# Low parts of split weights: a VectorE subtraction, or a ScalarE copy and an accumulating transfer

## The chip, the cores and the metric

The kernel runs on one core of a Trainium2 chip. The metric is the device time of one execution in microseconds. Three runs of the kernel before took 1647.87, 1644.26 and 1647.29 us, median 1647.29. A core has TensorE (matmuls, PE in the profile, its weight loads PEld), VectorE (DVE), ScalarE (ACT), GpSimd (POOL) and SyncE (SP), each working through its own queue of instructions in order, and 16 DMA engines, which all queues of transfers share.

## The reference

A two-layer backbone over 512 latent tokens and 256 context tokens of width 1024, batch 1, in float32. Around every sub-layer stand RMS norms with a shift, a scale and a gate taken from a conditioning vector (adaLN).

```python
h = rmsnorm(x, norm_g[l, 0]) * (1.0 + sc1) + sh1          # latent, and context with its own shift and scale
# layer 0: z = h @ w_in; multi-scale pooling heads beside a two-way gated linear recurrence (HGRN2); concat @ w_out
# layer 1: grouped-query attention, 8 query heads on 2 key heads, normalised q and k, 2-D rotary positions; @ w_out
x = x + g1 * rmsnorm(y, norm_g[l, 1])
a, b = split((rmsnorm(x, norm_g[l, 2]) * (1.0 + sc2) + sh2) @ ffn_w_in[l])
x = x + g2 * rmsnorm((silu(a) * b) @ ffn_w_out[l], norm_g[l, 3])
```

The context stream is needed up to the keys and values of layer 1; the output is the latent stream, 512 x 1024. The FFN's hidden width is 2816.

## The kernel before

Activations lie transposed: channels on the 128 partitions, tokens along the columns. Large products are computed from split operands. Each float32 operand is held as two float32r tiles, a rounded one ("hi") and the rest ("lo"), and a product is the sum of three matmuls, hi·hi, hi·lo of the activation, and lo·hi of the weight (`mm3`, lines 121 to 123). TensorE needs both parts of a weight before it can finish a product.

Weights come in slots of 128 x 2048 (`wslot`). For each half slot of 128 x 1024 (512 KB), SP loads the raw weights into one of four `raw` tiles (line 102), ScalarE copies them, rounded, into the hi tile (line 573), and VectorE subtracts hi from raw into the lo tile (line 574, in `split`). Slots live in a pool of two (`whi`, `wlo`); in the FFNs every third slot goes to a third place (`w3hi`, `w3lo`), and the output projections have two more (`wohi`, `wolo`). There are 92 slots: the value projection of layer 0 (2), its input projection (10), its output projection (4), the FFN of layer 0 (33), the projections of layer 1 (6 with the values), its output projection (4), and the last FFN (33). A slot can be filled again only when TensorE has made its last matmul from it; a `raw` tile can be loaded again only when its reader is done.

```python
hi = pool.tile([128, 2048], F32R, tag=tag + "hi", name=tag + "hi")
for a in range(0, n, 1024):
    self.split(hi[:, a:b], lo[:, a:b], self.load(src[:, a:b], b - a)[:, :b - a], self.weng)
```

`split` is also used for activations (attention's keys, queries, probabilities, the FFN's hidden tiles); those calls are not touched.

The program is written stage after stage, with norms of the next stage let in between the matmuls of the last (`along`, `tick`). Norm chains (`sumsq`, `rms`, `spread`, `postnorm`, `prenorm`) run from ScalarE's squares over VectorE's sums (line 171), a small TensorE matmul (140), GpSimd's power (146) and a second small matmul (158) to VectorE's products (187, 229). GpSimd also adds the gated result to x (233) and, at the start, makes half of the low parts of the modulated input (215). The order of instructions on each engine is then set by the framework's scheduler, which goes by its own estimate of when operands are ready, and which adds the waits; so an edit in one place can change the order of all engines. During the FFN of layer 0, 48 further loads through the `raw` tiles feed the adaLN products of layer 1 on VectorE (line 299); during the mixer of layer 0, 32 such loads feed TensorE (line 277). SP's queue also carries the rotary transfers of layer 1 (`sw`, line 677).

Of the kernel before, what the change touches and what calls it, by code (L numbers as in the profile page):

```python
# [12 lines left out]
ALU = mybir.AluOpType  # L13
# [37 lines left out]
class Cols:  # L51
    """Tiles of context (256) and latent (512) columns by channel tile, addressed by column 0..768."""
# [8 lines left out]
class Groups:  # L61
    """256-column tiles by channel tile."""
# [19 lines left out]
class Trunk:  # L82
# [22 lines left out]
    def wslot(self, src, n, pool=None, tag="w"):  # L105
        """One slot of weights, split into two parts that add up to it exactly."""
        if pool is None:
            self.nw += 1
            pool, tag = (self.w3, "w3") if self.w3 and self.nw % 3 == 0 else (self.wp, "w")
        hi = pool.tile([128, 2048], F32R, tag=tag + "hi", name=tag + "hi")  # L110
        lo = pool.tile([128, 2048], F32R, tag=tag + "lo", name=tag + "lo")
        for a in range(0, n, 1024):
            b = min(n, a + 1024)
            self.split(hi[:, a:b], lo[:, a:b], self.load(src[:, a:b], b - a)[:, :b - a], self.weng)
        return hi, lo

    def mm3(self, out, ops, first=True, last=True):
        """Sum over k of w_k^T x_k from split operands (wh, wl, xh, xl)."""
        n = len(ops)
        for i, (wh, wl, xh, xl) in enumerate(ops):  # L120
            self.nc.tensor.matmul(out=out, lhsT=wh, rhs=xh, start=first and i == 0, stop=False)  # L121
            self.nc.tensor.matmul(out=out, lhsT=wh, rhs=xl, start=False, stop=False)  # L122
            self.nc.tensor.matmul(out=out, lhsT=wl, rhs=xh, start=False, stop=last and i == n - 1)  # L123
# [5 lines left out]
    def ops(self, w, o, h, a, b, k0=0, k1=KD):  # L129
        """Operands of mm3: blocks k0..k1 of weights from column o on against h's columns a..b."""  # L130
        return [(w[0][:, o + (k - k0) * 128:o + (k - k0 + 1) * 128], w[1][:, o + (k - k0) * 128:o + (k - k0 + 1) * 128],
                 h[0](k, a, b), h[1](k, a, b)) for k in range(k0, k1)]

    def rms(self, ss, n, count, tag="aux"):
        """rsqrt(sum over partitions of ss / count + eps) by column."""
        nc = self.nc
        nt = n // 128
        pc = self.ps(tag)
        for t in range(nt):
            nc.tensor.matmul(out=pc[:, 2 * t:2 * t + 2], lhsT=ss[:, t * 128:(t + 1) * 128], rhs=self.ones[:, 0:2],  # L140
                             start=True, stop=True)
        v = self.sm.tile([128, 6], F32, tag="rv", name="rv")
        nc.vector.tensor_scalar(out=v[:, :nt], in0=pc.rearrange("p (t two) -> p t two", two=2)[:, :nt, 0],  # L143
                                scalar1=1.0 / count, scalar2=EPS, op0=ALU.mult, op1=ALU.add)
        r = self.sm.tile([128, 6], F32, tag="rr", name="rr")
        nc.gpsimd.tensor_tensor(out=r[:, :nt], in0=v[:, :nt], in1=self.mhalf[:, :nt], op=ALU.pow)  # L146
        return r, n

    def spread(self, rn, tag="aux"):
        """What rms returned, on every partition: PSUM [128, n]."""  # L150
        nc = self.nc
        r, n = rn
        dg = self.sm.tile([128, 256], F32, tag="dg", name="dg")
        for t in range(n // 128):
            nc.vector.tensor_scalar(out=dg[:, t * 128:(t + 1) * 128], in0=self.ident, scalar1=r[:, t:t + 1],
                                    scalar2=None, op0=ALU.mult)
        pb = self.ps(tag)
        nc.tensor.matmul(out=pb[:, :n], lhsT=self.ones, rhs=dg[:, :n], start=True, stop=True)  # L158
        return pb
# [16 lines left out]
    def prenorm(self, x, h, l, which, a, b):  # L176
        """h = rmsnorm(x) * (1 + sc) + sh of the columns a..b (of one stream), in two parts."""
# [21 lines left out]
    def norm(self, x, a, b):  # L199
        """x = rmsnorm(x) without its gain, over the columns a..b."""  # L200
        ss = yield from self.sumsq(x, a, b)
        rb = self.spread(self.rms(ss, b - a, D))
        for k in range(KD):
            self.nc.vector.tensor_tensor(out=x(k, a, b), in0=x(k, a, b), in1=rb[:, :b - a], op=ALU.mult)

    def modulate(self, x, h, l, which, a, b):
        """h = x * (1 + sc) + sh of the columns a..b (of one stream) of a normalised x, in two parts."""
# [10 lines left out]
    def postnorm(self, x, y, l, which, a, b):  # L218
        """x += gate * rmsnorm(y) over the columns a..b (of one stream)."""
# [20 lines left out]
    def tick(self, us):  # L240
        """Emit the next parts of what goes along, for us of the main work."""
        self.credit = min(self.credit, 0.0) + us * RATE
        while self.bg and self.credit > 0:
            try:
                self.credit -= next(self.bg[0][1])
            except StopIteration:
                self.bg.pop(0)

    def advance(self, n=1):
        """Emit the next step of what waits for it."""  # L250
        for _ in range(n):
            self.pend = [g for g in self.pend if next(g, 0) is None]
# [5 lines left out]
    def finish(self, key=None):  # L258
        """Emit the rest of what goes along up to key (all of it without)."""
        while self.bg and (key is None or key in [k for k, _ in self.bg]):  # L260
            for _ in self.bg.pop(0)[1]:
                pass
# [19 lines left out]
    def ada_steps(self, n):  # L282
        """The next n of the steps that are left, which fill in between other work."""
# [10 lines left out]
    def ada_cols(self, m):  # L294
        """One tile of 128 columns of the modulation for both streams, by rows of the transposed weights."""
# [13 lines left out]
    def ada_tail(self, l, m0, m1, src):  # L309
        """Tiles m0..m1 of the modulation from what src has without the bias, and what follows from them."""  # L310
# [17 lines left out]
    def zslots(self, h, idx, evac):  # L328
        """Two 128-channel tiles of the input projection of layer 0 from one slot of weights."""
# [9 lines left out]
    def mixer0(self, hx, mx):  # L339
# [5 lines left out]
        def z_evac(h, d):  # L345
            """d = 0 forward, 1 backward: forget gates f (rows backward, forward) and k = 1 - f (forward, backward)."""
# [34 lines left out]
        def mixed(t, c):  # L381
            """[p, n, half, c] of a tile of two rows: the lower half of each block of 2c columns from the first row,
            the upper half from the second."""
# [3 lines left out]
        def hgrn(h):  # L387
            # Products of forget gates within blocks of c columns, c doubling: Q holds q times the product from the
            # block's start (forward) or to its end (backward), K holds k times the product of the rest of the block.
            # The pairs that meet at level c lie in the two halves of a block of 2c.  # L390
# [12 lines left out]
            def amm(kt, qt, w):  # L403
                """Products of the blocks of w columns: block g's keys with the columns qt(g), side by side by chunk."""
# [103 lines left out]
        def u_evac(g):  # L508
            w = POOL_WINDOWS[g]

            def f(pt, a, b):
# [4 lines left out]
                # columns: pad, context, pad, latent, pad  # L516
# [59 lines left out]
    def put(self, mx, k, s, e, src, scale=None):  # L576
        """Split src (times a column) into the operand tiles mx, columns s..e."""
# [23 lines left out]
    def ffn(self, l, y, h, order0, groups, last, done, step=0):  # L601
        """y = (silu(h w_a) * (h w_b)) w_out, hidden tiles in chunks; order0: the (tile, group) pairs to start with;
        the last chunk goes by the groups of last, each followed by done."""
# [67 lines left out]
    def rope(self, t, s):  # L671
        """Rotary positions of t [128, n], in place; s: its columns of the latent."""
# [9 lines left out]
    def att_proj(self, h, yp):  # L682
        """Queries (rotated, not yet normalised), their scales, and split keys and values."""
# [81 lines left out]
    def attention(self):  # L765
# [17 lines left out]
        def scores(u):  # L783
            """Softmax of 128 queries of a head over all keys."""
# [211 lines left out]
    def setup(self, cp):  # L996
# [20 lines left out]
        # lower bounds: row 0 of the softmax over the two rows  # L1017
# [20 lines left out]
def _cols(v):  # L1038
    """(..., n*128) -> [128, ... n]"""
# [4 lines left out]
def _tiles(w, cols):  # L1044
    """The 128-wide column tiles of w [K, N] named by cols: [len(cols), 128 p, K/128, 128]"""
# [5 lines left out]
def _pair(t):  # L1051
    """[2m, 128, k, 128] -> [m, 128, 2*k*128]"""
# [4 lines left out]
def pack(inp):  # L1057
# [5 lines left out]
    # ada: [l, sb, k, p, j, tile, 32]  # L1063
# [53 lines left out]
    # rotary tables: by channel of the head and latent token  # L1117
# [22 lines left out]
```

## Time and profile before

| | |
|---|---|
| runs | 1647.87, 1644.26, 1647.29 us; median 1647.29 |
| profiled execution, span from first to last instruction | 1643.8 us |
| TensorE busy | 1573.1 us (96%) |
| VectorE, ScalarE, GpSimd busy | 946.9, 587.2, 116.6 us |
| mean granted TensorE clock | 0.987 |
| read from HBM | 158.35 MB |
| DMA engines busy with queue 1 (SP's) | 31.7% of 16 engines |

The page gives no time of the profiled execution beside its span; the span lies 0.5 us below the fastest of the three runs and 3.5 us below their median. A busy share is an average over stages: in the attention, VectorE and ScalarE are nearly full, in the FFNs they are half idle. In the timelines a row gives start, duration, engine, line, the tiles written and read, and in brackets how long the engine sat idle before it and what ended that.

### The profile page before, as it was taken

The numbers are of one execution on the slowest core, as the hardware profiler recorded it, in microseconds if no ns is written. First come the engines' busy times: TensorE is split into PE (matmuls) and PEld (weight loads), VectorE is DVE, ScalarE is ACT, GpSimd is POOL, SyncE is SP. The second block draws the span as 40 slices with busy tenths as digits, with TensorE's granted clock in tenths as the row PEclk, the third lists the DMA queues.
The fourth block names the chain that finished last, engine by engine and source line by source line (L and its number), as shares of the span: only waits on it lengthen the run. The fifth ranks groups of instructions, "written<-read, shape, count | busy, mean of one in ns | idle before, by whom it ended". The sixth has DMA issues, their size and how long they took to land.

```text
span 1643.8 us, 26760 instructions
## 1 busy us (share of the span) xinstructions
PE 1573.1 (96%) x10842; PEld 1375.0 (84%) x10842; DVE 946.9 (58%) x1899; ACT 587.2 (36%) x1104; POOL 116.6 (7%) x147
## 2 busy tenths in 40 slices
PE   4999999999999999999999999999999999999997
PEld 1877776789898888888888898889998888888886
DVE  5557676655756566676532458778937523343345
ACT  3424343254542211212122134548845332222222
POOL 0200000001210000000000012320003000000002
PEclk9999999999999999999999999999999999999998
DMA  9242232342215444444321213230032223322311
GB/s 337 79 155 78 80 128 79 122 134 92 97 56 162 129 144 151 141 143 153 129 72 57 62 42 103 72 110 27 2 103 78 89 91 102 103 92 88 103 52 52
DMA packets 55803, 167.95 MB, mean 102 GB/s; under 512 B 7040, under 2 KB 16000, under 8 KB 55296
## 3 DMA queue, kind: packets, MB, share of 16 engines
q1 hardware_dynamic: 55536, 166.05, 31.7%
q8 instruction: 85, 1.39, 0.3%
q14 instruction: 38, 0.31, 0.1%
q10 hardware_dynamic: 144, 0.20, 0.0%
HBM read 158.35 MB, written 5.24 MB: 100 GB/s over the span
## 4 chain that ended last, share of the span: by engine, by line
PE 67%; DVE 5%; POOL 2%; issue 1%; ACT 1%; SPq 0%; DMA 0%; POOLq 0%; DVEq 0%; ACTq 0%
PE mm L121 21%; PE mm L122 21%; PE mm L123 21%; PE pp L819 1%; DVE ss L171 1%; DVE u L229 1%; PE aux L158 1%; POOL xl L233 1%; PE st L121 1%; PE st L123 1%; PE aux L140 1%; PE st L122 1%; POOL rr L146 1%; DVE wlo L574 1%; SPq L677 0%
## 5 line engine op out<-in xcount | busy, mean ns | idle before, releaser
L121 PE MATMUL mm<-hhl,whi 128*128 128x512 f32 (+1 forms) x944 | 326.8, 348 | 4.9 <-ACT kt L732 3.7
L123 PE MATMUL mm<-hhl,wlo 128*128 128x512 f32 (+1 forms) x944 | 326.8, 347 | 0.0
L122 PE MATMUL mm<-hll,whi 128*128 128x512 f32 (+1 forms) x944 | 326.4, 347 | 0.0
L573 ACT ACTIVATE whi<-raw 128x1024 fp32r<-128x1024 f32 x132 | 135.4, 1054 | 306.0 <-PE mm L122 243.7
L121 PEld LDWEIGHTS mm<-hhl,whi 128*128 128x128 f32 x944 | 180.1, 192 | 25.6 <-ACT kt L732 3.9
L123 PEld LDWEIGHTS mm<-hhl,wlo 128*128 128x128 f32 x944 | 180.3, 191 | 20.3
L122 PEld LDWEIGHTS mm<-hll,whi 128*128 128x128 f32 x944 | 180.6, 192 | 19.3
L624 DVE TENSOR_TENSOR sa<-sa,mm 128x512 f32<-128x512 f32 (+1 forms) x76 | 40.9, 539 | 270.0 <-PE mm L123 269.9
L574 DVE TENSOR_TENSOR wlo<-raw,whi 128x1024 fp32r<-128x1024 f32 x132 | 160.4, 1236 | 57.5 <-ACT whi L573 54.3
L146 POOL TENSOR_TENSOR rr<-rv,mhalf 128x2 f32<-128x2 f32 x55 | 45.6, 834 | 1471.8 <-DVE rv L143 1469.1
L299 DVE SCALAR_TENSOR_TENSOR junk<-raw,cb 128x1024 f32<-128x1024 f32 x96 | 117.3, 1222 | 44.4 <-DMA raw<-adat 43.5
L639 DVE TENSOR_TENSOR y<-y,mm 128x256 f32<-128x256 f32 x200 | 76.8, 417 | 90.5 <-PE mm L123 90.0
L123 PE MATMUL mm<-hhl,w3lo 128*128 128x512 f32 (+1 forms) x336 | 117.4, 350 | 0.0
L121 PE MATMUL mm<-hhl,w3hi 128*128 128x512 f32 (+1 forms) x336 | 117.4, 350 | 0.0
L122 PE MATMUL mm<-hll,w3hi 128*128 128x512 f32 (+1 forms) x336 | 117.2, 349 | 0.0
L121 PE MATMUL mm<-ghl,whi 128*128 128x512 f32 (+1 forms) x304 | 111.2, 371 | 1.3 <-DVE sa L624 1.3
L122 PE MATMUL mm<-gll,whi 128*128 128x512 f32 (+1 forms) x304 | 112.0, 370 | 0.4 <-DVE gll L574 0.4
L123 PE MATMUL mm<-ghl,wlo 128*128 128x512 f32 (+1 forms) x304 | 111.0, 367 | 0.0
L121 PE MATMUL mm<-hhc,whi 128*128 128x256 f32 x384 | 110.3, 291 | 0.1
L123 PE MATMUL mm<-hhc,wlo 128*128 128x256 f32 x384 | 109.5, 287 | 0.0
L122 PE MATMUL mm<-hlc,whi 128*128 128x256 f32 x384 | 108.3, 284 | 0.2 <-issue 0.2
L623 ACT ACTIVATE sa<-mm 128x512 f32<-128x512 f32 (+1 forms) x76 | 36.5, 480 | 159.0 <-PE mm L123 158.7
(227 smaller groups left out, 3319.1 us busy)
## 6 DMA issues: line engine op xcount, KB each, us to landing
raw<-w_fi SPq DMA_DIRECT2D x88, 512.0 KB, 3.9
raw<-ada SPq DMA_DIRECT2D x48, 512.0 KB, 5.3
raw<-adat SPq DMA_DIRECT2D x48, 512.0 KB, 3.7
raw<-w_fo SPq DMA_DIRECT2D x44, 512.0 KB, 4.0
raw<-w_ab SPq DMA_DIRECT2D x20, 512.0 KB, 4.4
raw<-w_at SPq DMA_DIRECT2D x10, 512.0 KB, 4.5
xl<-x SPq DMA_DIRECT2D x16, 256.0 KB, 5.2
raw<-w_abo SPq DMA_DIRECT2D x8, 512.0 KB, 4.3
```

Of the source, the lines that this page charges most:

```text
L121: self.nc.tensor.matmul(out=out, lhsT=wh, rhs=xh, start=first and i == 0, stop=False)
L122: self.nc.tensor.matmul(out=out, lhsT=wh, rhs=xl, start=False, stop=False)
L123: self.nc.tensor.matmul(out=out, lhsT=wl, rhs=xh, start=False, stop=last and i == n - 1)
L140: nc.tensor.matmul(out=pc[:, 2 * t:2 * t + 2], lhsT=ss[:, t * 128:(t + 1) * 128], rhs=self.ones[:, 0:2], start=True, stop=True)
L146: nc.gpsimd.tensor_tensor(out=r[:, :nt], in0=v[:, :nt], in1=self.mhalf[:, :nt], op=ALU.pow)
L158: nc.tensor.matmul(out=pb[:, :n], lhsT=self.ones, rhs=dg[:, :n], start=True, stop=True)
L299: nc.vector.scalar_tensor_tensor(out=self.junk, in0=raw, scalar=1.0, in1=self.cb[:, i * 1024:i * 1024 + 1024], op0=ALU.mult, op1=ALU.mult, ...
L573: self.nc.scalar.activation(out=hi, in_=src, func=AF.Copy)
L574: (eng or self.nc.vector).tensor_tensor(out=lo, in0=src, in1=hi.bitcast(F32), op=ALU.subtract)
L623: nc.scalar.activation(out=s[:, :n], in_=p[0][:, :n], func=AF.Silu)
L624: nc.vector.tensor_tensor(out=s[:, :n], in0=s[:, :n], in1=p[1][:, :n], op=ALU.mult)
L639: nc.vector.tensor_tensor(out=yt, in0=yt, in1=p, op=ALU.add)
```

## The change

In `wslot`, the low part of a half slot is made in another way. ScalarE writes a second copy of the raw weights, times -1, into the lo tile, rounded like the hi tile; then GpSimd issues a transfer inside SBUF from `raw` to `lo` that adds what it reads to what is there. The call of `split` is gone from `wslot`, and VectorE has no part in the weights any more. The other lines of the diff only remove comments; what follows `wslot` has line numbers higher by 3.

```diff
         for a in range(0, n, 1024):
             b = min(n, a + 1024)
-            self.split(hi[:, a:b], lo[:, a:b], self.load(src[:, a:b], b - a)[:, :b - a], self.weng)
+            raw = self.load(src[:, a:b], b - a)[:, :b - a]
+            self.nc.scalar.activation(out=hi[:, a:b], in_=raw, func=AF.Copy)
+            self.nc.scalar.activation(out=lo[:, a:b], in_=raw, func=AF.Copy, scale=-1.0)
+            self.nc.gpsimd.dma_start(out=lo[:, a:b], in_=raw, accum_op=ALU.add)
         return hi, lo
```

ScalarE's queue ahead of the value projection of layer 0, before; `hhc` are the rounded tiles of the modulated input:

```order
L573 ACTIVATE whi<-raw 128x1024
L214 ACTIVATE hhc_113<-u 128x256
L214 ACTIVATE hhc_114<-u 128x256
L214 ACTIVATE hhc_115<-u 128x256
L573 ACTIVATE whi<-raw 128x1024
L214 ACTIVATE hhc_116<-u 128x256
L214 ACTIVATE hhc_117<-u 128x256
L573 ACTIVATE whi<-raw 128x1024 x2
```

The same place now:

```order
L115 ACTIVATE whi<-raw 128x1024
L116 ACTIVATE wlo<-raw 128x1024
L115 ACTIVATE whi<-raw 128x1024
L116 ACTIVATE wlo<-raw 128x1024
L115 ACTIVATE whi<-raw 128x1024
L116 ACTIVATE wlo<-raw 128x1024
L115 ACTIVATE whi<-raw 128x1024
L116 ACTIVATE wlo<-raw 128x1024
L217 ACTIVATE hhc_113<-u 128x256
```

All eight weight copies now stand ahead of the first copy of the input, where one stood before.

GpSimd's queue at the same place now; before, the low parts `hlc` followed the powers at once:

```order
L149 TENSOR_TENSOR rr<-rv,mhalf 128x2 x3
L117 DMA wlo<-raw 128x1024 x4
L218 TENSOR_TENSOR hlc_130<-u,hhc_114 128x256
L218 TENSOR_TENSOR hlc_132<-u,hhc_116 128x256
L218 TENSOR_TENSOR hlc_134<-u,hhc_118 128x256
```

Four issues, each waiting for its second copy, now stand between the powers and the input's low parts.

TensorE's queue at the first slot of the FFN of layer 0, before (`w3hi`, `w3lo` are the slot's two parts):

```order
L158 MATMUL aux<-dg,ones 128x256
L121 MATMUL mm<-hhc_3727,w3hi 128x256
L122 MATMUL mm<-hlc_3743,w3hi 128x256
L123 MATMUL mm<-hhc_3727,w3lo 128x256
L121 MATMUL mm<-hhc_3728,w3hi 128x256
```

The same place now:

```order
L161 MATMUL aux<-dg,ones 128x256
L124 MATMUL mm<-hhc_3751,w3hi 128x256
L125 MATMUL mm<-hlc_3767,w3hi 128x256
L124 MATMUL mm<-hhc_3751,w3hi 128x256
L125 MATMUL mm<-hlc_3767,w3hi 128x256
L124 MATMUL mm<-hhl_3759,w3hi 128x256
L125 MATMUL mm<-hll_3775,w3hi 128x256
L124 MATMUL mm<-hhl_3759,w3hi 128x256
L125 MATMUL mm<-hll_3775,w3hi 128x256
L126 MATMUL mm<-hhc_3751,w3lo 128x256
```

The first matmul that reads the low part now comes after eight that don't, where two stood before; the matmuls of three further products have been drawn ahead.

## Rows read from the trace of the kernel before

**Rows 1.** The page: span, and busy time of each engine with its share.
```profile
span 1643.8 us, 26760 instructions
PE 1573.1 (96%) x10842; PEld 1375.0 (84%) x10842; DVE 946.9 (58%) x1899; ACT 587.2 (36%) x1104; POOL 116.6 (7%) x147
```

**Rows 2.** Instructions of the split by line: count, ns min/median/max, first and last start.
```profile
L573 ACT ACTIVATE whi<-raw x132: 1039/1058/1092, 37.7 to 1594.6; 128x1024 fp32r<-128x1024 f32 x132
...
L574 DVE TENSOR_TENSOR wlo<-raw,whi x132: 1184/1224/1760, 40.8 to 1595.9; 128x1024 fp32r<-128x1024 f32 x132
...
L574 DVE TENSOR_TENSOR w3lo<-raw,w3hi x44: 1216/1220/1226, 433.8 to 1585.0; 128x1024 fp32r<-128x1024 f32 x44
...
L574 DVE TENSOR_TENSOR wolo<-raw,wohi x8: 1215/1225/1227, 359.3 to 1206.3; 128x1024 fp32r<-128x1024 f32 x8
```

**Rows 3.** Timeline, last FFN: a slot's subtractions, and TensorE's first read of them.
```profile
1365.35 2.36 DVE L574 TENSOR_TENSOR wlo<-raw,whi 128x1024 fp32r<-128x1024 f32 x2
...
1386.72 0.39 PE L123 MATMUL mm<-ghl,wlo 128*128 128x512 f32 x1
```

**Rows 4.** The page's DMA queue 1, and DMA issues (count, size, us to landing).
```profile
q1 hardware_dynamic: 55536, 166.05, 31.7%
...
raw<-w_fi SPq DMA_DIRECT2D x88, 512.0 KB, 3.9
...
raw<-w_abv SPq DMA_DIRECT2D x4, 512.0 KB, 10.2
...
sw<-y SPq DMA_DIRECT2D x64, 32.0 KB, 1.9
```

**Rows 5.** Three stretches: us, busy time (count) by engine, PEclk, DMA share, GB/s.
```profile
0.00:40.00 40.00, 18.46 (x84) 6.02 (x84) 21.84 (x72) 15.18 (x33) 2.57 (x8) 0.96 0.93 345
354.00:434.00 80.00, 77.18 (x610) 74.32 (x610) 47.77 (x99) 44.90 (x98) 15.73 (x20) 1.00 0.41 139
1290.00:1605.00 315.00, 315.00 (x1466) 263.01 (x1465) 118.41 (x165) 85.27 (x116) 0.00 (x0) 1.00 0.30 94
```

**Rows 6.** Timeline, five places: rounded copies, and TensorE's first read of the low part.
```profile
74.99 2.01 ACT L573 ACTIVATE whi<-raw 128x1024 fp32r<-128x1024 f32 x2 [2.17 <-PE mm L123]
...
77.70 0.30 PE L123 MATMUL mm<-hhc,wlo 128*128 128x256 f32 x1
...
90.98 2.24 ACT L573 ACTIVATE whi<-raw 128x1024 fp32r<-128x1024 f32 x2 [0.50 <-DMA raw<-w_ab]
...
96.78 0.28 PE L123 MATMUL mm<-hhc,wlo 128*128 128x256 f32 x1
...
432.55 1.05 ACT L573 ACTIVATE w3hi<-raw 128x1024 fp32r<-128x1024 f32 x1
433.50 0.51 ACT L190 ACTIVATE hhl<-u,mods 128x256 fp32r<-128x256 f32 x1
...
435.04 0.38 PE L123 MATMUL mm<-hhc,w3lo 128*128 128x256 f32 x1 [0.89 <-DVE w3lo L574]
...
1027.15 1.06 ACT L573 ACTIVATE whi<-raw 128x1024 fp32r<-128x1024 f32 x1 [1.28 <-PE mm L122]
...
1031.26 0.28 PE L123 MATMUL mm<-hhl,wlo 128*128 128x256 f32 x1
...
1255.17 1.05 ACT L573 ACTIVATE w3hi<-raw 128x1024 fp32r<-128x1024 f32 x1
...
1259.37 0.28 PE L123 MATMUL mm<-hhl,w3lo 128*128 128x256 f32 x1
```

**Rows 7.** Timeline, the start: ScalarE's first weight copy and input copies, TensorE's first low-part wait.
```profile
37.68 1.06 ACT L573 ACTIVATE whi<-raw 128x1024 fp32r<-128x1024 f32 x1 [12.62 <-DMA raw<-w_abv]
...
39.15 1.06 ACT L214 ACTIVATE hhc<-u 128x256 fp32r<-128x256 f32 x3 [0.41 <-DVE u L212]
...
42.03 1.22 PE L122 MATMUL mm<-wlo,hhc 128*128 128x512 f32 x2 [1.68 <-DVE wlo L574]
```

**Rows 8.** Timeline, TensorE at the seam of FFN and layer 1.
```profile
1011.73 0.47 PE L140 MATMUL aux<-ones,ss 128*128 128x2 f32 x3 [2.24 <-DVE ss L171]
```

## The prediction, made before the changed kernel was run

> **What bounds the kernel now.** I read the busy shares first, then the split's own groups, then the timeline of each place where a split weight is first used. TensorE is busy for 1573.1 of the 1643.8 us of the span [rows 1]: the reader should see that any change can win at most the 71 us in which it is not, and that 21.5 of these lie in the first 40 us [rows 5], ahead of the first weight matmul, where no split has been needed yet. VectorE (947 us) and ScalarE (587 us) are far from full, so taking work from one and giving it to the other is worth nothing by itself. What counts is when a rounded weight or its low part becomes ready against when TensorE first reads it.
>
> The split is done 132 + 44 + 8 = 184 times, each on a half slot of 128x1024: a ScalarE copy of about 1.05 us, then a VectorE subtraction of about 1.22 us [rows 2]. In the steady part of the last FFN, the subtraction of a half slot starts at 1365.35 and takes 2.36 us with its neighbour, while TensorE reads the first half only at 1386.72 [rows 3]: some 20 us to spare. In the first FFN it is more. So most of the 92 slots can become ready several us later without anybody noticing. A few cannot, and they carry the forecast.
>
> **The change part by part.**
> Removed: 184 subtractions on VectorE, 184 x 1.22 = 224 us of busy time. Added on ScalarE: 184 further copies of the same shape as the rounded one, 184 x 1.05 = 193 us, which brings it to 780 us, below half of the span. Added on GpSimd: 184 DMA issues, in order with its own additions and powers. Added on the DMA engines: 184 transfers of 512 KB that read the raw weights and add to what lies in the low tile.
>
> *The price of one transfer.* No row of before shows an accumulating transfer, nor one issued by GpSimd. Nearest rows: a 32 KB transfer inside SBUF lands 1.9 us after its issue, a 512 KB load lands in 3.9 us, and in 10.2 us where four stand in a full queue [rows 4]. All of queue 1, 166.05 MB, takes 31.7% of 16 engines, which is 0.317 x 1643.8 / 166.05 x 0.524 = 1.65 us of all engines for 512 KB. The result needs two operands through the engines, the raw weights and minus the rounded ones, so I take two passes: 1.9 + 2 x 1.65 = 5.2 us, and 0.4 us for the issue, like SP's at its issues: 5.6 us in all. Lower bound 1.9 us, upper bound 10.6 us.
>
> On the price the Trainium skill says something too. In "DMA: Bandwidth & Descriptors", section "Anatomy of one DMA — SWDGE (gpsimd) path", it puts a GpSimd DMA at 2.0 us plus bytes over 436 GB/s, which is 3.2 us here, an estimate by that page; its term agrees with the 1.9 us of the small transfer [rows 4]. By it the sum below would shrink to almost nothing. The same page, under "Rules for kernel authors", says that an accumulating DMA reads its destination and writes it later, which no run here shows yet, and which would speak for the second pass.
>
> *The places with no room.* New ready time = end of the rounded copy + 1.06 us (the second copy) + 5.6. Against it stands TensorE's first read of the low part, later by what the new order puts in between, at 315.00 / 1466 = 0.215 us for a 512-column matmul and 77.18 / 610 = 0.127 us for a 256-column one [rows 5]. All from [rows 6]:
> - First slot of the input projection. Its buffer's minus copy now goes ahead of the rounded one, so 74.99 + 1.06 + 5.6 = 81.65; first read 77.70 + 7 x 0.215 = 79.2. Late by 2.4.
> - Second slot: 90.98 + 1.06 + 6.66 = 98.7 against 96.78. Late by 1.9.
> - First slot of the first FFN (the third weight pool, which reuses the space of the output projection, so nothing can be prepared earlier): 432.55 + 1.05 + 6.66, and a 0.5 us activation that the new order sets between the copies, 440.75; first read 435.04 + 6 x 0.127 = 435.8. Late by 4.9. TensorE already waits 0.89 us there for the subtraction.
> - The keys' slot of layer 1: 1027.15 + 1.06 + 6.66 = 1034.9 against 1031.26 + 10 x 0.127 = 1032.5. Late by 2.3.
> - First slot of the last FFN: 1255.17 + 1.05 + 6.66 = 1262.9 against 1259.37 + 3 x 0.127 = 1259.75. Late by 3.1.
> Ten places are of this kind; these five are the first, the last, and the ones with least room. Between them lie two more slots of the input projection, two of the first output projection and one of the query projection, late by 0.4 to 2.1 each, 5.8 together by the same sum. Ten places: 14.6 + 5.8 = 20.4 us. The second half of a slot follows 2 us after the first and is read 2 to 20 us later, so it adds nothing. Every other slot has more room than 6 us and costs nothing; its cover is TensorE working on the slots before it, and that is gone as soon as a transfer takes longer than that room.
>
> *The start.* The raw weights of the value projection land at 37.68, and the first activation of the modulated input runs at 39.15, between the copies [rows 7]. In the new order all eight copies stand ahead of it: 37.68 + 8 x 1.06 = 46.2, 7.0 us later. VectorE gives some of it back, since four subtractions of 1.22 us no longer stand between its steps there, and TensorE's wait of 1.68 us for the first low part is gone. GpSimd's additions for that input also stand behind four issues. I take +5, bounds 2 and 9.
>
> *What is given back.* At the seams between stages, norm chains run over VectorE with subtractions in between; the largest gap of TensorE at such a seam is 2.24 us, at 1011.73 [rows 8], right behind three of them. I take -3 for all seams, bounds 0 and -4.8. What is late next there: GpSimd's additions to x, now with issues between them.
>
> *The clock.* Where TensorE idled, the granted clock of the stretch fell: 0.96 over the first 40 us against 1.00 in the two later stretches [rows 5]. A new wait can bring a stretch at 1.2 GHz, in which work takes twice as long; I take +2 in all, bounds 0 and 7.
>
> *Raw buffers.* A raw tile is now held until its transfer has landed, about 5 us longer, so SP's next load, and the adaLN loads and rotary transfers queued behind it, go out later. In the FFNs loads go out some 15 to 20 us ahead of the copy, so this costs nothing there.
>
> Sum: 20.4 + 5 - 3 + 2 = +24.4 us on the profiled span of 1643.8, or 1668. The runs' median, 1647.29, lies 3.5 us above that span, so I predict 1672.
>
> **The rivals.**
> *The transfers become the bound.* Loads keep the DMA engines busy for 0.30 of the 315 us from 1290 to 1605 [rows 5], and nearly all of that is weights. Transfers of k passes bring it to 0.30 x (1 + k): 0.90 at two, and over 1 from k = 2.33 on. At three passes these 315 us become 378, +63, and the late places grow by 1.65 each to 37: 63 + 37 + 5 - 3 + 2 = +104, 1751 us. For it: nothing shows the rate of an accumulation. Against it: two passes still fit.
> *A cheap transfer, no change.* If the operand in place costs no pass of its own and the issue no time, 1.9 + 1.65 = 3.55 us; the late places shrink by 2.05 each to 4.6 us, and with the start at +2 and the seams at -4.8 the sum is +1.8: 1649 us. For it: 1.9 us for the small transfer. Against: four places keep next to no room. The page's 3.2 us above would end here.
> *Faster.* The seams decide. If the transfer lands in 1.9 us, only the first FFN's slot is late (1.2), the start costs nothing because VectorE, not ScalarE, sets it, and the seams give their 4.8 and the 1.7 of the start: -5, 1642 us. It decides as soon as a transfer takes less than 2.6 us. Against it: 512 KB alone is 1.65 us of engine time.
>
> **How the numbers follow.** Forecast 0.55 (own range 1655 to 1695); transfers as the bound 0.22; no change 0.14; faster 0.09. About 0.2% (3.3 us) is what a measurement of this kernel can tell from no change. Faster: 0.09 and 0.01 of the cheap case, 0.10; same: the rest of the cheap case, 0.13; slower: 0.55 + 0.22 = 0.77. The range leaves the fastest tenth out below 1646 and reaches past three passes to 1760.
>
> **What would show it.** Right: waits of TensorE for the low weight tiles at some ten places, 2 to 5 us each, the largest at the first FFN's first slot; the first weight matmul some 5 us later; transfers that land in 5 to 6 us; DMA busy near 0.9 in the last FFN with TensorE still full. Wrong: a landing time under 3 us, or a last FFN in which TensorE waits at every slot, or GpSimd issues of over 2 us that delay its additions at the seams.

## The result, and the profile after

The changed kernel takes 1727.83 us (median of 4, 1725.32 to 1728.89), the kernel before 1645.78 us beside it: a ratio of 1.0495, 95% interval 1.0482 to 1.0508. That is 82 us slower. The direction was forecast; the size, +24, was less than a third of it.

The page of the changed kernel: span, busy times, the two large DMA queues (packets, MB, share of 16 engines), GpSimd's issues, and landings (count, KB each, us from issue to landing).

```profile
span 1726.7 us, 27162 instructions
...
PE 1601.2 (93%) x10842; PEld 1392.0 (81%) x10842; DVE 750.3 (43%) x1715; ACT 753.4 (44%) x1288; POOL 265.4 (15%) x331
...
q0 software_dynamic: 26496, 96.48, 30.4%
q1 hardware_dynamic: 55536, 166.05, 29.3%
...
L117 POOL DMA_DIRECT2D wlo<-raw x132 | 115.3, 874 | 806.9 <-ACT wlo L116 615.0
...
wlo<-raw POOLq DMA_DIRECT2D x132, 512.0 KB, 5.2
raw<-w_fi SPq DMA_DIRECT2D x88, 512.0 KB, 4.5
...
w3lo<-raw POOLq DMA_DIRECT2D x44, 512.0 KB, 5.6
```

Against [rows 1], VectorE has 197 us less to do and ScalarE 166 us more. TensorE runs the same 10842 matmuls, yet is busy 28.1 us longer; the other 54.8 us of the longer span are time in which it is not busy. Its waits, all groups added up, went from 61.9 to 114.0 us. The larger ones, as us in total, times, longest:

```profile
PE aux L161 <- DVE dg L158: 19.7, 24, 3.4
PE aux L143 <- DVE ss L174: 19.7, 7, 13.0
PE mm L124 <- ACT ghl L576: 17.8, 4, 9.2
PE mm L126 <- DMA wlo<-raw: 13.3, 7, 5.0
PE mm L124 <- ACT hhc L217: 7.6, 1, 7.6
PE mm L126 <- DMA w3lo<-raw: 4.8, 3, 4.0
...
PE mm L124 <- ACT wohi L115: 3.0, 2, 1.6
PE mm L125 <- DMA wlo<-raw: 2.8, 2, 1.9
PE mm L126 <- DMA wolo<-raw: 2.8, 3, 1.3
PE mm L124 <- ACT w3hi L115: 2.5, 2, 1.9
```

The four groups on a low part add up to 23.7 us in 15 waits. The third line is the one that no step of the forecast had: TensorE waits for `ghl`, the rounded hidden activations of the FFN, which are no weights at all. Three of its four waits, 17.5 us, lie in the first FFN.

The chain of waits that ends at the longest of these, at 550.36 (start, us, what):

```profile
524.62 9.45 DMA wlo<-raw
534.07 0.02 SPq L102
...
534.13 5.07 DMA raw<-adat
...
539.33 1.25 DVE junk L302 x2
...
541.86 4.59 DMA raw<-adat
...
546.54 1.25 DVE junk L302 x2
...
549.04 0.61 DVE sa L627
549.68 0.64 ACT ghl L576
550.36 0.79 PE mm L124
```

It reads like this. A raw buffer, one of the ring of four `raw` tiles, is held until an accumulating transfer has landed, 9.45 us after its issue. Only then can SP load the next block of adat into it. VectorE, which works in order, has adat's products (`junk`) in front of `sa`; `sa` feeds `ghl`, and TensorE stands still for 9.22 us. VectorE's wait for adat was 43.5 us in the kernel before and is 117.6 now (the kernel before, then the changed one). That total is a sign and not the price: e5 below has 123.7 us of it and next to no wait for `ghl`. What counts is when the products ahead of this one `sa` get their data.

```profile
DVE junk L299 <- DMA raw<-adat: 43.5, 31, 3.5
```
```profile
DVE junk L302 <- DMA raw<-adat: 117.6, 36, 11.7
```

The same place in stretches of 5 us (busy time of each engine, then PEclk and DMA share):

```profile
535.00:540.00 5.00, 5.00 (x29) 4.40 (x28) 0.67 (x1) 2.01 (x2) 0.24 (x1) 1.00 0.74 250
540.00:545.00 5.00, 1.14 (x6) 0.60 (x4) 4.26 (x8) 0.00 (x0) 0.62 (x1) 0.94 0.93 215
545.00:550.00 5.00, 0.00 (x0) 0.00 (x0) 3.07 (x5) 0.32 (x1) 0.00 (x0) 0.50 0.47 158
550.00:555.00 5.00, 4.64 (x17) 3.97 (x18) 1.62 (x2) 3.14 (x7) 0.86 (x1) 0.53 0.86 252
555.00:560.00 5.00, 5.00 (x29) 4.35 (x28) 1.54 (x4) 1.30 (x4) 0.00 (x0) 1.00 0.64 143
```

The granted clock falls to 0.50 (1.2 GHz) while TensorE waits, and is still there for some 4 us after the wait has ended: a 512-column matmul takes 0.79 us at 550.36 and 0.39 us at 556.30. A wait of 9.2 us delays what stands behind it by 11.3 us: by the measure of the table below the delay is 32.2 us ahead of it and 43.5 behind.

At the mixer's out-projection the ring shows again. SP's last two loads of `w_abo` go out from 386.92 on, where the kernel before issued its last one at 365.99; 12.6 us of that are the delay with which this stretch begins. Both the low part ahead of these loads and the rounded copy behind them are late at TensorE. (SP, then ScalarE, then TensorE; the last row is the first slot of the first FFN.)

```profile
386.92 3.31 SPq L102 DMA_DIRECT2D raw<-w_abo  x2
```
```profile
394.15 1.06 ACT L115 ACTIVATE wohi<-raw 128x1024 fp32r<-128x1024 f32 x1 [2.92 <-DMA raw<-w_abo]
```
```profile
383.55 0.39 PE L126 MATMUL mm<-hhc,wlo 128*128 128x256 f32 x1 [3.84 <-DMA wlo<-raw]
...
395.26 0.39 PE L124 MATMUL mm<-hhc,wohi 128*128 128x256 f32 x1 [1.57 <-ACT wohi L115]
...
466.17 0.58 PE L126 MATMUL mm<-hhc,w3lo 128*128 128x256 f32 x1 [4.02 <-DMA w3lo<-raw]
```

The steady part of the last FFN was forecast rightly: DMA share 0.84, TensorE full, against 0.30 in [rows 5].

```profile
1371.00:1686.00 315.00, 314.66 (x1462) 262.13 (x1462) 50.17 (x105) 140.53 (x175) 51.29 (x60) 1.00 0.84 194
```

Where the time went, as the delay in us against the kernel before: each instruction of a ScalarE line against the one with the same number in that line, median over a stretch. The heads give the stretch, in us of the kernel before.

```
run                       80-200   345-364   430-445   445-500   740-960 1110-1190 1210-1255 1330-1500
changed kernel              12.1      12.6      25.1      32.2      57.2      76.2      79.1      80.8
e1  add from HBM            23.2      28.0      44.2      55.0      71.7      88.8      92.1      93.2
e2  no adat loads            8.2       9.2      21.5      30.3      35.9      53.0      56.2      63.2
e3  second copy only         3.1       6.5       9.3      10.5      11.0      12.3      12.6      11.5
e4  eight columns            3.3       1.6       4.5       7.9       9.2       8.9       9.0       4.8
e5  add rounded part        21.5      22.0      35.3      44.3      50.4      67.1      71.5      73.1
e9  bytes, no waits         11.5      15.0      27.3      28.1      43.0      57.1      57.1      56.2
e10 three in a row          21.4      27.5      43.9      56.1      88.5     106.8     112.7     116.5
e11 ring of five            15.0      17.1      32.0      40.3      81.9      98.5     101.0     101.9
```

The columns are: the mixer, its last slots, the end of its out-projection; the first FFN's first slots, and its end; layer 1's attention, its out-projection; the last FFN. The changed kernel loses 25 us up to 445 (half of it by the mixer's first slots, half at its out-projection), 7 at the first FFN's first slot, 25 in the rest of that FFN, 22 around layer 1's attention, and nothing once the last FFN is under way.

### The profile page after: what moved, and what is told of

Its sections match the earlier page's. It is cut to its first block, busy times and chain, and to the rows that moved or that the text cites. A ratio compares the mean times of both kernels' runs of the same rounds, so it can differ in the third digit from the quotient of the medians.

```text
span 1726.7 us, 27162 instructions
## 1 busy us (share of the span) xinstructions
PE 1601.2 (93%) x10842; PEld 1392.0 (81%) x10842; DVE 750.3 (43%) x1715; ACT 753.4 (44%) x1288; POOL 265.4 (15%) x331
## 3 DMA queue, kind: packets, MB, share of 16 engines
q0 software_dynamic: 26496, 96.48, 30.4%
## 4 chain that ended last, share of the span: by engine, by line
PE 62%; DMA 15%; issue 11%; DVE 6%; ACT 4%; POOL 2%; SPq 1%; POOLq 0%; DVEq 0%; ACTq 0%
PE mm L126 18%; PE mm L124 18%; PE mm L125 18%; DMA wlo<-raw 4%; DMA raw<-adat 2%; DMA w3lo<-raw 1%; DVE junk L302 1%; DMA wolo<-raw 1%; PE pp L822 1%; DMA xc<-x 1%; PE aux L161 1%; DMA sw<-y 1%; ACT wlo L116 1%; PE aux L413 1%; POOL rr L149 1%
## 5 line engine op out<-in xcount | busy, mean ns | idle before, releaser
L115 ACT ACTIVATE whi<-raw 128x1024 fp32r<-128x1024 f32 x132 | 139.0, 1054 | 292.1 <-PE mm L125 179.8
L117 POOL DMA_DIRECT2D wlo<-raw x132 | 115.3, 874 | 806.9 <-ACT wlo L116 615.0
L302 DVE SCALAR_TENSOR_TENSOR junk<-raw,cb 128x1024 f32<-128x1024 f32 x96 | 117.5, 1224 | 119.4 <-DMA raw<-adat 117.6
L116 ACT ACTIVATE wlo<-raw 128x1024 fp32r<-128x1024 f32 x132 | 138.3, 1047 | 1.9 <-PE mm L125 1.9
L124 PE MATMUL mm<-ghl,whi 128*128 128x512 f32 (+1 forms) x304 | 112.7, 376 | 18.7 <-ACT ghl L576 17.5
L174 DVE TENSOR_TENSOR ss<-ss,sq 128x256 f32<-128x256 f32 x147 | 69.8, 479 | 68.3 <-ACT sq L173 62.1
```

The lines of the kernel that those rows point to most:

```text
L115: self.nc.scalar.activation(out=hi[:, a:b], in_=raw, func=AF.Copy)
L116: self.nc.scalar.activation(out=lo[:, a:b], in_=raw, func=AF.Copy, scale=-1.0)
L117: self.nc.gpsimd.dma_start(out=lo[:, a:b], in_=raw, accum_op=ALU.add)
L174: nc.vector.tensor_tensor(out=ss[:, :n], in0=ss[:, :n], in1=sq[:, :n], op=ALU.add)
L302: nc.vector.scalar_tensor_tensor(out=self.junk, in0=raw, scalar=1.0, in1=self.cb[:, i * 1024:i * 1024 + 1024], op0=ALU.mult, op1=ALU.mult, ...
```

## The experiments

Three theories stood at the outset. A: the raw buffers, held longer, starve the ring. B: the transfer itself, by its landing at the readers and by its bytes. C: ScalarE's second copy and the new order.

**e1, the addend read from HBM.** The raw buffer is free as soon as ScalarE has read it.

```diff
-self.nc.gpsimd.dma_start(out=lo[:, a:b], in_=raw, accum_op=ALU.add)
+self.nc.gpsimd.dma_start(out=lo[:, a:b], in_=src[:, a:b], accum_op=ALU.add)
```


> The changed kernel, but the accumulating transfer takes the weights a second time from HBM instead of from the raw buffer; as many bytes are added, and the raw buffer is free once ScalarE's two copies have read it. Theory A (the ring): of the 82 us lost, most comes from raw buffers that are held until the low part has landed (5 to 10 us longer), so that the ring of four feeds later loads late: the ghl waits of the first FFN (17.8 us of waits, 25 us of delay with the half-clock stretches behind them), the late out-projection of the mixer (about 13 us of delay) and part of the projections of layer 1 (17 us). Then this run takes 1665 to 1695 us, and no ghl wait in the first FFN is above 2 us. Theory B (the transfer itself: its bytes and its landing time): nothing is gained, 1720 to 1745 us. Theory C (ScalarE's second copy): nothing is gained, 1720 to 1735 us.

1743.13 us, ratio 1.0596 (1.0567 to 1.0624): slower still, inside B's range. A's number failed. But the `ghl` wait fell from 17.8 to 3.4 us, while the first FFN's transfers now land in 9.4 us instead of 5.2 and the low parts are late by 47.1 us in all instead of 23.7. Two effects moved against each other, so this run settles neither.

**e2, no adat loads in the first FFN.**

```diff
-        raw = self.load(self.a["adat"][m], 1024)
-            ...scalar_tensor_tensor(out=self.junk, in0=raw, ...
+            ...scalar_tensor_tensor(out=self.junk, in0=self.cb[:, :1024], ...
```


> The changed kernel without the 48 loads of adat in the first FFN: VectorE's 96 products read cb in place of them, so the modulation of layer 1 is left out, and VectorE's work stays. Theory A (the ring, and through it adat's loads that VectorE waits for ahead of sa): the three ghl waits (9.2, 3.9 and 4.4 us) go, with the half-clock stretches behind them; the rest stays: 1700 to 1708 us. Theory B (the low part lands late at its readers) and theory C (ScalarE's second copy ahead of ghl in ScalarE's order): the waits stay, 1722 to 1732 us.

1711.89 us, ratio 1.0413, 4 us above A's range and 10 below that of B and C; the `ghl` waits fall from 17.8 to 5.0 us. In the table the first FFN behind its first slots loses 5.6 us instead of 25.0, so adat's loads carry some 19 us there. The total shrinks by 16 only: of the gain, some 5 us are lost again ahead of the last FFN, and why was not looked into.

**e3, the kernel before with the second copy.**

```diff
+self.nc.scalar.activation(out=lo[:, a:b], in_=raw, func=AF.Copy, scale=-1.0)
 self.nc.vector.tensor_tensor(out=lo[:, a:b], in0=raw, in1=hi[:, a:b].bitcast(F32), op=ALU.subtract)
```


> The kernel before with ScalarE's second copy added (minus the raw weights into the low part, which VectorE's subtraction then writes over): ScalarE's work is that of the changed kernel, VectorE's that of the one before, no transfer. Theory A (the ring): the second copy costs little, as the buffer is held only about 1 us longer: 1646 to 1656 us. Theory C (ScalarE's second copy is what delays): most of the loss is there, 1690 to 1730 us. Theory B: 1644 to 1652 us.

1658.17 us, ratio 1.0081 (1.0058 to 1.0105), +14 us, a little above the ranges of A and B. Theory C is out for the large part.

**e4, a transfer of eight columns.**

```diff
-self.nc.gpsimd.dma_start(out=lo[:, a:b], in_=raw, accum_op=ALU.add)
+self.nc.gpsimd.dma_start(out=lo[:, a:a + 8], in_=raw[:, :8], accum_op=ALU.add)
```


> The changed kernel with the accumulating transfer cut to 8 of each half slot's 1024 columns: the addition is left out for the rest. GpSimd's issue and the wait for a landing stay, the bytes go, and the raw buffer is free some 3 us earlier. Theory A (the ring): most of the delay goes, 1655 to 1685 us. Theory B: the same, since both bytes and landing shrink; the two part at the run that adds from HBM. Theory C (ScalarE's second copy): 1715 to 1730 us.

1652.65 us, ratio 1.0051 (1.0036 to 1.0066). Second copy, issue and waits are all there, and so is the order of adat's products and `sa` in VectorE's queue. The 512 KB are gone, and with them half of the landing time and 73 of the 82 us, more than A and B expected. Bytes and a shorter hold go together here, so the run does not part A from B. Its transfers land in 2.7 us and the loads in 3.5 (the queue, and the landings):

```profile
q0 software_dynamic: 26496, 0.77, 2.5%
```
```profile
raw<-w_fi SPq DMA_DIRECT2D x88, 512.0 KB, 3.5
...
wlo<-raw POOLq DMA_DIRECT2D x132, 4.0 KB, 2.7
```

**e5, the rounded part as addend.** SBUF to SBUF and the same bytes, with the raw buffer free early.

```diff
-self.nc.gpsimd.dma_start(out=lo[:, a:b], in_=raw, accum_op=ALU.add)
+self.nc.gpsimd.dma_start(out=lo[:, a:b], in_=hi[:, a:b], accum_op=ALU.add)
```


> The changed kernel, but the accumulating transfer takes the rounded part (hi) as its source instead of the raw weights: the low part comes out as zero, and the transfer has the same bytes from SBUF to SBUF and the same waits at its readers, but the raw buffer is free once ScalarE's two copies have read it. Unlike the run that adds from HBM, no transfer becomes slower. Theory A (the ring of four raw buffers, held until the transfer lands): the first FFN's ghl stalls go (25 us of delay), and the part of the out-projection's and of layer 1's projections that comes from late loads (15 to 25 us): 1680 to 1702 us. Theory B (low parts that land late at their own readers, and bytes): 1720 to 1732 us.

1723.91 us, ratio 1.0492 (1.0471 to 1.0512): as slow as the changed kernel, so A as stated fell. The table shows why the total says too little. From 500 to 960 this run loses 6.1 us where the changed kernel loses 25.0; its `ghl` wait is 2.5 us. Adat's first load goes out 67 us after the FFN's first matmul, against 76 in the changed kernel and 58 in the one before, with as many products ahead of that `sa`. That stall is the held buffer, shown with the bytes unchanged. In exchange it loses 10 us more before 445: its transfers land in 8.0 us. That they meet loads which go out earlier is the likely reason, not one that a run separates (its landings, then TensorE's waits).

```profile
wlo<-whi POOLq DMA_DIRECT2D x132, 512.0 KB, 8.0
raw<-w_fi SPq DMA_DIRECT2D x88, 512.0 KB, 5.1
```
```profile
PE mm L126 <- DMA wlo<-whi: 20.2, 9, 3.6
...
PE mm L124 <- ACT ghl L576: 2.5, 1, 2.5
```

**e6, the eight columns plus bytes nobody waits for.**

```diff
 self.nc.gpsimd.dma_start(out=lo[:, a:a + 8], in_=raw[:, :8], accum_op=ALU.add)
+for _ in range(2):
+    ...   # o: the next of 16 places in dummy, which lies in HBM
+    self.nc.gpsimd.dma_start(out=self.dummy[:, o:o + b - a], in_=hi[:, a:b])
```


> The kernel of the eight columns (1652.65 us) and with each half slot two plain transfers of 512 KB from the rounded part to HBM, for which nothing waits: about the bytes and the engine time of the accumulating transfer (two at some 1.6 us of the sixteen DMA engines against 2.85), without its landing in anybody's way. If bytes on the DMA engines as such cost time (they slow the loads), it takes 1670 to 1700 us; if only the landing counts (at the readers of the low part, and in the ring), 1650 to 1662 us.

1716.38 us, ratio 1.0437, above both ranges. Inconclusive: the small transfers stand behind the large ones in the same queue, and SP waited 689.0 us for them, as for the transfers of the changed kernel (706.6). e9 asks again without them.

**e7 and e8, the change in one FFN only** (a flag in `wslot` chooses between the two ways).

```diff
+if self.moved:
+    ...   # the second copy and the transfer
+else:
+    ...   # VectorE's subtraction
```


> The kernel before, with the change made only in the last FFN (66 of the 184 half slots); VectorE subtracts elsewhere. All theories place next to none of the loss there (the delay stays at 80 us from 1285 us of the kernel before to its end): 1640 to 1650 us, and VectorE, with some 80 us less work around the last seam, may gain up to 4 us there.

> The kernel before, with the change made only in the first FFN (66 of the 184 half slots). If the first FFN's loss is made there (first slot 6.7 us, the three ghl stalls 25 us, by the delay against the kernel before), 1670 to 1682 us; if it depends on loads that came late before it, 1650 to 1662 us.

The last FFN alone: 1651.94 us, ratio 1.0042 (1.0027 to 1.0058), +7.8, 2 us above the range that was expected. By the measure of the table some 5 us arise in the seam to that FFN and its first slots and nothing behind them. No gain from VectorE's relief shows. The first FFN alone: 1675.43 us, ratio 1.0188, +31.3, with a `ghl` wait of 16.1 us. The first FFN's loss is made there.

**e9, the kernel before plus bytes nobody waits for.**

```diff
 self.split(hi[:, a:b], lo[:, a:b], ...)
+for _ in range(2):
+    ...   # o: the next of 16 places in dummy, which lies in HBM
+    self.nc.gpsimd.dma_start(out=self.dummy[:, o:o + b - a], in_=hi[:, a:b])
```


> The kernel before (VectorE subtracts) with two plain transfers of 512 KB from each half slot's rounded part to HBM added on GpSimd's queue; nothing waits for them. The kernel of the eight columns with the same bytes had its small transfers queued behind them, this one has no reader and no raw buffer behind them. Theory B1 (bytes as such: they slow the loads): 1670 to 1710 us. Theory B2 (the bytes cost only where a landing is waited for, by a reader or by the ring of raw buffers): 1644 to 1658 us.

1703.41 us, ratio 1.0364 (1.0349 to 1.038). So bytes alone cost too: loads of `w_fi` land in 6.8 us instead of 3.9, adat's in 7.8 instead of 3.7 (its landings, below). But these transfers are not those of the change: GpSimd's queue takes 32.0% of the engines against 30.4% in the changed kernel, it writes to HBM, and loads land later beside it than in the changed kernel (4.5). So 60 us is no measure of what the bytes cost there. TensorE waits for `ghl` for 2.9 us only, so slower loads alone do not make the stall at 550; but VectorE waits 121.7 us for adat, and the first FFN loses 14.9 us behind its first slots, with 5.6 us of waits for `y`, which VectorE writes too. Adat's loads are a way for lost time there in either case.

```profile
raw<-w_fi SPq DMA_DIRECT2D x88, 512.0 KB, 6.8
...
raw<-adat SPq DMA_DIRECT2D x48, 512.0 KB, 7.8
```

**e10, three small transfers in a row.**

```diff
-self.nc.gpsimd.dma_start(out=lo[:, a:b], in_=raw, accum_op=ALU.add)
+for _ in range(3):
+    self.nc.gpsimd.dma_start(out=lo[:, a:a + 8], in_=raw[:, :8], accum_op=ALU.add)
```


> The changed kernel with three accumulating transfers of 8 columns one after the other in place of the one of 1024 columns (the addition is left out for the rest): some 6 us from issue to the last landing as before, hardly any bytes; GpSimd stands in its queue for two of the landings. Theory A (the time for which the raw buffer is held, whatever the bytes): the first FFN loses 15 to 25 us between its first and its last chunk, and the whole takes 1690 to 1730 us. Theory B1 (bytes): the first FFN loses under 5 us there, 1652 to 1675 us.

1771.31 us, ratio 1.0764 (1.0734 to 1.0794), with next to no bytes (2.30 MB) and loads as quick as without the change (3.6 us). From the first issue to the last landing it takes 6.4 us in the median half slot, against 5.4 in the changed kernel; counted from the end of the second copy 8.5 against 5.8, as GpSimd stands in its own queue until the small transfers land. Delay without bytes costs more than the changed kernel does, far above the range of A: low parts are late and `ghl` is late. The run does not part the held buffer from GpSimd's queue, and VectorE's order differs a little too (TensorE's waits, then a landing).

```profile
PE mm L127 <- DMA wlo<-raw: 23.7, 10, 7.4
PE mm L125 <- ACT ghl L577: 21.4, 5, 5.9
```
```profile
raw<-w_fi SPq DMA_DIRECT2D x88, 512.0 KB, 3.6
```

**e11 and e12, a ring of five.**

```diff
-self.pool("raw", 4) as self.rawp
+self.pool("raw", 5) as self.rawp
-self.junk = self.gp.tile([128, 1024], F32, name="junk")
+self.junk = self.gp.tile([128, 1024], mybir.dt.uint8, name="junk")
```


> The changed kernel with five raw buffers in place of four (VectorE's thrown-away products are written as bytes to make room). Theory A: a fifth more loads can be under way, most of the ghl stalls of the first FFN go (25 us) and about a third of the late loads at the out-projection and in layer 1 (8 us): 1690 to 1705 us. Theory B (landing at the readers): 1715 to 1730 us; loads that go out earlier meet the transfers, as in the runs that freed the raw buffer early, and the landings get longer.

> The kernel before with five raw buffers in place of four: the control for the ring. Its waits for loads are short (no PE wait on a weight load above 2 us), so 1640 to 1648 us by every theory.

Both expectations failed: 1749.20 us (ratio 1.0643) and 1658.83 us (1.0096), each slower than with four. With a fifth buffer the order of VectorE's queue changes: at the first `ghl` wait of e12, 40 of adat's products stand ahead of that `sa`, where 36 stood with four buffers. That this is the reason is argued from the order; no run holds it fixed. VectorE's wait for them rises to 166.0 us, and to 95.4 in the kernel before, which now has `ghl` waits too (the ring of five in the kernel before, VectorE, then TensorE):

```profile
DVE junk L299 <- DMA raw<-adat: 95.4, 35, 4.7
```
```profile
PE mm L121 <- ACT ghl L573: 9.5, 2, 4.9
```

**h13 and h14, the change in the other stages only** (the flag of e7).

> The kernel before, with the change made only in the mixer and its out-projection (32 of the 184 half slots). By the delay of the changed kernel against the one before, 25 us have been lost by the end of that out-projection. If each stage loses by itself: 1664 to 1674 us. If the late loads are handed on from stage to stage: 1650 us or less, or 1680 us or more.

> The kernel before, with the change made only in the projections of layer 1 and their out-projection (20 of the 184 half slots). The changed kernel loses 24 us there (from 57 to 81 us of delay). If each stage loses by itself: 1660 to 1672 us; else 1650 us or less.

1674.13 us (ratio 1.0186, +30.6) and 1661.56 us (1.0107, +18.1). Both agree with a loss in each stage by itself (h13 at the upper edge of its range). With e8 and e7 the four stages give 30.6 + 31.3 + 18.1 + 7.8 = 87.8 us, against 82 for all together. Layer 1 shows a second small stream that no experiment was aimed at, the rotary transfers `sw` that stand in SP's queue behind the weights: VectorE waited 1.0 us for them in the kernel before and waits 22.8 in the changed one (21.5 in h14, but 3.1 in e4). What that costs TensorE was not separated (VectorE in the kernel before, then in the changed one).

```profile
DVE y L678 <- DMA sw<-y: 1.0, 1, 1.0
```
```profile
DVE y L681 <- DMA sw<-y: 22.8, 8, 6.2
```

**h15, the first FFN only, without adat's loads** (e8 with the edit of e2).

> The kernel with the change in the first FFN only (1675 us), without the 48 loads of adat (VectorE's products read cb; the modulation of layer 1 is left out). If the loss of the first FFN is that of adat's loads in the shared ring, which VectorE waits for ahead of sa: 1650 to 1658 us, the first slot's 7 us staying. If it is the weights' own landing: 1670 to 1676 us.

1659.92 us, ratio 1.0097, +16.4: 14.9 of e8's 31.3 us go with adat's loads, somewhat less than expected; by the measure of the table some 8 at the first slots and 5 behind them stay, a `ghl` wait of 3.1 us among them.

**h16, the minus copy first.** The second copy and the transfer's issue go ahead of the rounded copy.

> The changed kernel with ScalarE's minus copy ahead of the rounded copy, so that the transfer starts some 1.0 us earlier for each half slot, with the same work on every engine. The ring's turn gets about 1 us shorter of some 13: by the landing time (three small transfers in a row, the one of 1024 columns, the one of 8 columns: about 15 to 40 us lost for each us of hold) 1695 to 1725 us. If the bytes alone count, 1722 to 1732 us.

1720.80 us, ratio 1.0466 (1.0438 to 1.0494). That is inside the range given by the hold and just below that of the bytes alone. Its interval overlaps that of the changed kernel, so the 7 us between the medians are not settled; at most a small gain.

No run points to a version that beats the kernel before: where the transfer is free, in the steady last FFN, the subtraction was free as well.

## Why the prediction was wrong

*The price of one transfer: near.* 5.6 us were taken, issue included. A landing is counted from the start of the issue: 5.2 to 5.6 us, of which the issue is 0.87 rather than 0.4, and 10.1 where `wolo`'s come in a burst. The Trainium skill, "DMA: Bandwidth & Descriptors", section "Anatomy of one DMA — SWDGE (gpsimd) path", would have it land in 3.2 us, an estimate by that page; the 5.2 decides. The 1.9 us that the prediction took from [rows 4] was a transfer of SP's; GpSimd's 4 KB accumulation lands in 2.4 to 2.7 us (e4). In engine time a half slot is 0.304 x 1726.7 / 96.48 x 0.524 = 2.85 us, against 3.3 for two passes of a load.

*Low parts late at their readers: near in sum, and the sum by luck.* 20.4 us forecast, 23.7 measured in the rows above, with 2.6 in the kernel before [rows 6, 7]. The first FFN's first slot is late by 4.0 (4.9 forecast), the keys' slot of layer 1 by 2.6 (2.3). The other places do not fit: the input projection's slots wait 1.2 us in all (4.3 for two of them alone), the last FFN's first slot 0.8 (3.1), and what is missing there is made up by the query slots of layer 1, 5.7 us, the value projection, 2.8, and the last out-projection, 1.8. The longest wait, 5.0 us, is at a query slot and not at the first FFN. The mixer's out-projection waits 4.8 us for low parts and 3.0 more for rounded parts, which no term had: its four slots come in a burst, and the ring lets the last loads out late.

*The start: right.* TensorE's wait for `hhc` is 7.6 us against 2.2; the cause given, copies ahead of the input in ScalarE's order, stands, for e3 and e4 show 8.2 without the large transfer. As delay it is some 3 us there (the table's first column), within the bounds.

*The seams: nothing given back.* -3 was taken. The waits for `dg` rose from 14.4 to 19.7, those for `ss` fell from 24.9 to 19.7: no change in sum.

*Raw buffers: the step that failed.* The prediction said that in the FFNs loads go out some 15 to 20 us ahead of the copy, "so this costs nothing there". That is true of the weights. It is not true of adat's loads, named in the sentence before, which take their turn in the same ring of four and feed VectorE ahead of `sa`. In the first FFN this is 17.5 us of waits and 25.0 us of delay, where the prediction had nothing; e2 and e5 take it away, e8 shows it with the change in that FFN alone, and h15 takes it away again. A turn of a buffer, by the page's rows, was 3.9 + 1.06 + 1.22 = 6.2 us and became 4.5 + 2 x 1.05 + 5.2 = 11.8 (an estimate without its waits). The shortest turn of a weight's buffer in the traces, from the load's issue to the buffer's release, is 6.2 and 10.8 us; the median is 22.0 and 23.5, since most buffers wait for ScalarE anyway. So the longer turn bites only where loads come close together, as at this stall.

*The clock: the second step that failed.* +2 was taken, bounds 0 and 7. The same matmuls took 28.1 us more. The mean granted clock is 0.968 against 0.987, and where the rows were read closely, at 550, the half-clock stretch came with the wait and outlasted it. In its stretches at 1.2 GHz TensorE is busy for 78.4 us, against 31.1 in the kernel before; half of the difference, 24 us, is the clock's part of the 28.1, an estimate. With waits underrated, this term had to be as well.

Together: the forecast had 22.4 us of idle time (20.4 + 5 - 3) and 2 of clock; 54.8 and 28.1 were measured.

*The rivals.* Transfers as the bound had the number nearer (1751), but by luck, for its mechanism did not come: the last FFN is full at a DMA share of 0.84.

What stays open: up to 445 and around layer 1's attention a longer delay of each half slot (e10) and slower loads (e9) each cost time, and freeing the buffer early gains nothing there, while landings get longer (e5). How the 25 and 22 us there divide between them was not separated; the failed step is shown for the 25 us of the first FFN alone.

## What to carry to other kernels

A staging buffer that is held longer is paid for by everything that passes through its ring, not only by the data that it holds: look for the small streams that share it, and for what stands behind them in an in-order queue. Here, moving arithmetic onto the DMA engines cost nothing only where the ring had turns to spare, in the steady last FFN; at bursts of loads ahead of a stage, count turns as well as bytes. And price a long new TensorE wait with the half-clock stretch that came with it here.

## What the runs showed of the hardware that was not expected

An accumulating 512 KB transfer inside SBUF takes 2.85 us of the sixteen engines against 1.6 for a load, and its landing goes from 5.2 to 8.0 us with the rounded part as addend and the raw buffer free early (e5), to 9.4 with its addend from HBM (e1). Two plain 512 KB transfers to HBM on GpSimd's queue for each load lengthen SP's loads from 3.9 to 6.8 us (e9). That agrees with the Trainium skill, "DMA: Bandwidth & Descriptors", section "Rules for kernel authors": queues issued from different engines share the same sixteen DMA engines. A 4 KB accumulation still lands only after 2.4 to 2.7 us.
